# Moving the start of a transformer block's big on-chip tiles by up to 1,472 bytes

## The chip, the core and the metric

The kernel runs on one core of a Trainium2 chip. A core has a matrix engine (TensorE, PE in the profile, with its weight loads shown apart as PEld), a vector engine (VectorE, DVE), a scalar engine (ScalarE, ACT), a general engine (GpSimd, POOL), and a sync engine (SyncE, SP) that issues most of the DMA transfers. Matrix products read both operands from the on-chip memory (SBUF) and write to accumulators (PSUM). The metric is the time of one execution in microseconds, as the median of several runs.

## The reference

The reference is one decoder layer on 1,024 positions of width 1,024, in float32:

```python
h = rms_norm(x, ln_pre_mix[l])
proj = h @ w_in[l]
...
q, k = rope(q, pos), rope(k, pos)
pool_out = multi_scale_pool(u_pool, w_pool[l], pool_scale[l])
attn_out = dilated_attention(q, k, v).reshape(B, S, ATTN_WIDTH)
mix = jnp.concatenate([pool_out, attn_out], axis=-1) @ w_out[l]
x = x + rms_norm(mix, ln_post_mix[l])
h = rms_norm(x, ln_pre_ffn[l])
f = (jax.nn.silu(h @ w_gate[l]) * (h @ w_up[l])) @ w_down[l]
x = x + rms_norm(f, ln_post_ffn[l])
```

The mixer has twelve rotary attention heads of width 64, each under three window-and-stride patterns that are merged by their softmax denominators, and beside them four groups of trailing-window means. The channel mixer (the FFN) has 2,816 hidden channels.

## The kernel before

**Arithmetic.** Every float32 operand of a large product is split in two parts of a reduced float32 type, "high" and "low": ScalarE writes the high part, and VectorE or GpSimd the remainder. Each product is then three matrix products (`PASSES`: high·high, high·low, low·high). A tile of split data therefore holds rows of 512 numbers, 2,048 bytes, of which a matmul reads one row as its moving operand. In the profile's names the moving operand comes first and the weights (the stationary operand) second: `ps_s<-b,fw` moves a row of `b` past weights from `fw`.

**Stages.** (1) The input is loaded and split, and the first projections are made (to about 84 us). (2) Attention, pooling and the remaining projections are interleaved (to about 440 us): scores move `k` past `qh` and `ql`; ScalarE takes exponentials in tiles `pp`; PE transposes `pp` by an identity or a permutation (`idt`, `pmt`, line 279) and the result is split to `ptr`, which moves past the values `v`. (3) The output projection and two norms follow (to about 484 us). (4) Gate and up projections run as a seven-product scheme on 2×2 blocks of the data and of the weights (Strassen and Winograd), in eleven steps j: first a part of the work of steps 0 to 5 (`firsts`), then the rest (`seven`). (5) The down projection does the same (912 us on). Lines 1468 and 1469 name the moving operand of each product:

```python
SEVEN = {"P1": ("A11", "11", "pj"), "P6": ("S2", "T2", "o"), "P2": ("A12", "21", "pj"), "P7": ("S3", "T3", "o"),
         "P5": ("S1", "T1", "s"), "P4": ("A22", "T4", "o"), "P3": ("S4", "22", "s")}
```

"11", "21" and "22" are blocks of the activations themselves, in the tiles `b` (made by `block`, line 1336); T1 to T4 are differences of blocks, in the tiles `tT`. One product of a step, lines 1560 to 1569, is 2 × 4 × 3 = 24 matmuls with 512 columns. `firsts` (lines 1367 to 1400) computes P1 and P2 of steps 0 to 5, 48 matmuls a step. So `b` moves in P1 and P2 in `firsts`, in P3 of every step, and in P1 and P2 of steps 6 to 10.

**Rooms in SBUF.** Tiles come from pools stacked from two ends. Pools without a side grow from the low (left) end: `const`, `wpool` (raw weights `wraw`), `small`, then `con1` and `att` (the attention's `pp`, `ptr`, `v`, `low`, `mix`, early `xraw`, and the last pool weights, `w`); when those two are closed, `ffnl` takes their place and begins where `con1` began (`b`, `rw` for raw FFN weights, `q`, `r3`, and at the end `xe` and half of the result). Pools with `side="right"` grow from the high end: `xg` (`x`, then `z`, `tT`, `op`), `hlp` (`whl`), `qkp` (`k`, `qh`, `ql`), later `mid` (`fw`, `sq`, `p`). Within a pool the big tiles are multiples of 2,048 bytes, so one offset of the pool's start decides the place of all of them within 2,048 bytes.

**Order.** A list of numbers (`PRM`) sets in which order steps are written, and a scheduler puts the instructions of each engine in a fixed order at build time. Each engine works through its own order and waits on semaphores.

Of the kernel before, what the change touches and what calls it, by code (L numbers as in the profile page):

```python
# [8 lines left out]
F32 = mybir.dt.float32  # L9
# [6 lines left out]
P = 128  # L16
# [254 lines left out]
def hybrid_block(ctx: ExitStack, tc: tile.TileContext, xT, w_in, w_v, w_vp, w_pool, w_out, w_gate, w_up, w_down,  # L271
                 g1, g2, g3, g4, pscale, cost, sint, maskA, maskB, quadA, quadB, lsel, ident, perm, band, out):
    nc = tc.nc
# [7 lines left out]
    const = ctx.enter_context(tc.tile_pool(name="const", bufs=1))  # L281
# [19 lines left out]
    def cload(src, shape, name, pool=None, eng=nc.sync):  # L301
        t = (pool or const).tile(shape, F32, name=name)
        eng.dma_start(t, src)
        return t
# [48 lines left out]
    con1 = left.enter_context(tc.tile_pool(name="con1", bufs=1))  # L353
# [8 lines left out]
    for h in range(2):  # L362
        for a in range(2):
            nc.gpsimd.memset(qlow[h][64 - 64 * a:128 - 64 * a, a].bitcast(F32), 0.0)
    ones = const.tile([P, 1], F32, name="ones")
    nc.vector.memset(ones, 1.0)
    warm = qkp.tile([P, 512], F32R, name="warm", tag="rsw", bufs=1)
    nc.vector.memset(warm.bitcast(F32), 0.0)
# [645 lines left out]
        did(("pool", h))  # L1014

    g2s, g3s, g4s = (cload(g, [P, NK], "g%ds" % (n + 2)) for n, g in enumerate((g2, g3, g4)))
    psc = cload(pscale, [P, 2], "psc", con1)

    def emit(*lists):

# [904 lines left out]
```

## Time and profile before

| | |
|---|---|
| median of 3 runs | 1139.48 us (1139.41 to 1140.89) |
| the profiled execution's own time | 1139.3 us |
| its span, first to last instruction | 1137.5 us |
| PE busy | 1120.4 us, 98% of the span |
| weight loads (PEld) | 958.1 us, 84% |
| DVE, ACT, POOL busy | 71%, 49%, 48% |
| granted PE clock over the span | 0.997 |

The profiled execution spends 1.8 us outside its span. Matmuls overlap in the array, so the duration of one (some 390 ns for 512 columns) is longer than the interval from its start to the next one's start, and it is the interval that costs time. The chain of waits lists the work that ended last, piece by piece, with a start, a length and a count; where PE runs without a break, the length divided by the count is that interval.

### The profile page before, as it was taken

The numbers are of one execution on the slowest core, as the hardware profiler recorded it, in microseconds if no ns is written. First come the engines' busy times: TensorE is split into PE (matmuls) and PEld (weight loads), VectorE is DVE, ScalarE is ACT, GpSimd is POOL, SyncE is SP. The second block draws the span as 40 slices with busy tenths as digits, with TensorE's granted clock in tenths as the row PEclk, the third lists the DMA queues.
The fourth block names the chain that finished last, engine by engine and source line by source line (L and its number), as shares of the span: only waits on it lengthen the run. The fifth ranks groups of instructions, "written<-read, shape, count | busy, mean of one in ns | idle before, by whom it ended". The sixth has DMA issues, their size and how long they took to land.

```text
span 1137.5 us, 16902 instructions
## 1 busy us (share of the span) xinstructions
PE 1120.4 (98%) x5922; PEld 958.1 (84%) x5922; DVE 807.6 (71%) x1516; ACT 559.1 (49%) x1068; POOL 550.6 (48%) x481
## 2 busy tenths in 40 slices
PE   9999999999999999999999999999999999999997
PEld 7888999999898888888888878888888888888896
DVE  7967888888998675989777777665676473343684
ACT  7466667666678573965422222322323434344441
POOL 0122646253465222010267667775577897666521
PEclk9999999999999999999999999999999999999999
DMA  8215242414147555773566666433544796566442
GB/s 280 93 70 186 83 141 75 149 57 167 56 131 246 181 200 193 291 254 123 188 231 231 232 231 231 167 141 142 190 167 167 272 351 222 192 203 192 141 149 74
DMA packets 91156, 201.59 MB, mean 177 GB/s; under 512 B 9280, under 2 KB 25152, under 8 KB 89664
## 3 DMA queue, kind: packets, MB, share of 16 engines
q1 hardware_dynamic: 90096, 199.74, 50.2%
q8 instruction: 46, 0.75, 0.3%
q10 hardware_dynamic: 976, 0.79, 0.2%
q14 instruction: 38, 0.31, 0.1%
HBM read 143.61 MB, written 56.89 MB: 176 GB/s over the span
## 4 chain that ended last, share of the span: by engine, by line
PE 87%; DVE 6%; POOL 3%; DMA 2%; issue 1%; ACT 1%; SPq 0%; ACTq 0%; DVEq 0%; POOLq 0%
PE ps_pj L276 28%; PE ps_s L276 25%; PE ps_o L276 22%; PE ps_t L276 10%; PE ps_t L279 3%; DMA rw<-in_w_up_dram 1%; POOL fw L1365 1%; POOL pp L814 1%; DVE pp L748 1%; DVE ptr L860 1%; DVE rsw L510 0%; POOL whl L1464 0%; DMA wraw<-in_w_in_dram 0%; ACT pp L751 0%; DVE ql L542 0%
## 5 line engine op out<-in xcount | busy, mean ns | idle before, releaser
L276 PE MATMUL ps_o<-tT,fw 128*128 128x512 f32 x648 | 150.9, 390 | 0.9 <-DVE sq L1548 0.9
L276 PEld LDWEIGHTS ps_o<-tT,fw 128*128 128x128 f32 x648 | 121.5, 188 | 26.9 <-issue 1.3
L276 PE MATMUL ps_pj<-x,whl 128*128 128x512 f32 x480 | 138.1, 407 | 0.3 <-DVE whl L322 0.3
L814 POOL TENSOR_SCALAR pp<-pp,wv 128x256 f32<-128x256 f32 (+1 forms) x135 | 67.8, 523 | 111.5 <-DVE wv L794 111.5
L1365 POOL TENSOR_TENSOR fw<-rw,fw 128x512 fp32r<-128x512 f32 x72 | 100.3, 1416 | 30.2 <-ACT fw L1363 30.1
L751 ACT ACTIVATE pp<-pp,sx 128x128 f32<-128x128 f32 (+1 forms) x192 | 89.3, 468 | 31.5 <-DVE sx L748 30.9
L276 PEld LDWEIGHTS ps_pj<-x,whl 128*128 128x128 f32 x480 | 85.0, 189 | 11.2 <-DVE whl L322 0.7
L348 POOL TENSOR_TENSOR nrr<-nrr,half 128x4 f32<-128x4 f32 (+1 forms) x7 | 7.9, 1124 | 145.5 <-ACT eps L347 103.8
L1660 POOL TENSOR_TENSOR op<-rw,op 128x512 fp32r<-128x512 f32 x38 | 62.3, 1638 | 32.5 <-ACT op L1659 32.5
L322 POOL TENSOR_TENSOR whl<-wraw,whl 128x512 fp32r<-128x512 f32 x42 | 54.7, 1327 | 45.3 <-ACT whl L318 45.3
L276 PE MATMUL ps_s<-b,fw 128*128 128x512 f32 x312 | 74.6, 394 | 0.0
L276 PEld LDWEIGHTS ps_s<-b,fw 128*128 128x128 f32 x312 | 58.5, 187 | 14.2
L1365 POOL TENSOR_TENSOR whl<-rw,whl 128x512 fp32r<-128x512 f32 x30 | 47.1, 1589 | 44.2 <-ACT whl L1363 30.1
L276 PE MATMUL ps_pj<-whl,x 128*128 128x256 f32 (+1 forms) x432 | 68.4, 299 | 0.0
L1363 ACT ACTIVATE fw<-rw 128x1024 fp32r<-128x1024 f32 x45 | 47.5, 1061 | 41.8 <-PE ps_o L276 17.8
L1659 ACT ACTIVATE op<-rw 128x1024 fp32r<-128x1024 f32 x38 | 40.0, 1058 | 56.4 <-PE ps_t L276 28.2
L860 DVE TENSOR_TENSOR ptr<-ps_t,ptr 128x512 fp32r<-128x512 f32 (+1 forms) x84 | 55.3, 665 | 12.1 <-ACT ptr L859 11.3
L859 ACT ACTIVATE ptr<-ps_t 128x512 fp32r<-128x512 f32 (+1 forms) x84 | 47.4, 578 | 27.9 <-PE ps_t L279 24.0
L276 PEld LDWEIGHTS ps_pj<-whl,x 128*128 128x128 f32 x432 | 58.2, 191 | 1.7
L1661 DVE TENSOR_TENSOR op<-rw,op 128x512 fp32r<-128x512 f32 x33 | 28.8, 872 | 40.1 <-ACT op L1659 29.9
L276 PE MATMUL ps_o<-ptr,v 128*128 128x128 f32 (+1 forms) x472 | 56.4, 257 | 0.2 <-DVE ptr L860 0.2
L276 PE MATMUL ps_s<-k,qh 128*128 128x128 f32 (+1 forms) x192 | 54.4, 295 | 1.9 <-DVE sx L748 1.5
(328 smaller groups left out, 2858.7 us busy)
## 6 DMA issues: line engine op xcount, KB each, us to landing
rw<-bd SPq DMA_DIRECT2D x77, 256.0 KB, 4.0
rw<-in_w_gate_dram SPq DMA_DIRECT2D x28, 512.0 KB, 4.3
rw<-in_w_up_dram SPq DMA_DIRECT2D x28, 512.0 KB, 5.9
v<-vd SPq DMA_DIRECT2D x22, 512.0 KB, 4.6
rw<-wsd SPq DMA_DIRECT2D x44, 256.0 KB, 3.8
bd<-p SPq DMA_DIRECT2D x39, 256.0 KB, 2.1
rw<-in_w_down_dram SPq DMA_DIRECT2D x33, 256.0 KB, 3.8
wraw<-in_w_out_dram SPq DMA_DIRECT2D x15, 512.0 KB, 4.8
```

The source lines that it names most:

```text
L276: return tc.keep_in_program_order(nc.tensor.matmul(*a, **k))
L279: return tc.keep_in_program_order(nc.tensor.transpose(dst, src, by))
L322: pin(eng.tensor_tensor(dst[:, 1, at:at + w], src[:, at:at + w], dst[:, 0, at:at + w].bitcast(F32), ALU.subtract))
L751: nc.scalar.activation(pt[:, j, lo:], pt[:, j, lo:], AF.Exp, bias=sx[:, 0, side, j, hd, 0:1], scale=-1.0, accum_out=sx[:, 0, side, j, hd, ...
L814: nc.gpsimd.tensor_scalar(pv, pv, un.wv[:, side, j, hd:hd + 1], 1.0, op0=ALU.mult, op1=ALU.mult)
L859: nc.scalar.activation(ptr[:, 0, :w], t[:, :w], AF.Copy)
L860: nc.vector.tensor_tensor(ptr[:, 1, :w], t[:, :w], ptr[:, 0, :w].bitcast(F32), ALU.subtract)
L1363: nc.scalar.activation(dst[:, :, 0], src, AF.Copy)
L1365: low[0] = eng.tensor_tensor(dst[:, i, 1], src[:, i], dst[:, i, 0].bitcast(F32), ALU.subtract)
L1659: nc.scalar.activation(w[:, :, 0], raw, AF.Copy)
L1660: nc.gpsimd.tensor_tensor(w[:, 0, 1], raw[:, 0], w[:, 0, 0].bitcast(F32), ALU.subtract)
L1661: (nc.gpsimd if p == "P1" else nc.vector).tensor_tensor(w[:, 1, 1], raw[:, 1], w[:, 1, 0].bitcast(F32), ALU.subtract)
```

## The change

Two small tiles become longer: `ones`, in the pool `const`, from 4 to 1,092 bytes in each partition, and `psc`, in `con1`, from 8 to 392 bytes. Only the first columns are used, as before. The load of `psc` is written out because the helper would load the whole tile; it is the same transfer of 2 numbers at the same place in SP's order.

```diff
-    ones = const.tile([P, 1], F32, name="ones")
+    ones = const.tile([P, 273], F32, name="ones")[:, :1]
     nc.vector.memset(ones, 1.0)
...
-    psc = cload(pscale, [P, 2], "psc", con1)
+    psc = con1.tile([P, 98], F32, name="psc")[:, :2]
+    nc.sync.dma_start(psc, pscale)
```

In the built program no instruction is added, removed or moved on any engine, and every wait is the same. What differs is addresses. All that lies behind `ones` on the left moves up by 1,088 bytes, and all that lies behind `psc` in `con1` and `att` by 384 bytes more. Bytes beyond a multiple of 2,048 at which the tiles begin:

| tiles | side | before | after |
|---|---|---|---|
| `b`, `rw`, `q`, `r3`, `xe` (pool `ffnl`) | left | 928 | 2,016 |
| `pp`, `ptr`, `v`, `xraw`, `w` (pool `att`) | left | 544 | 2,016 |
| `low`, `mix` (pool `att`) | left | 1,568 | 992 |
| `wraw` | left | 832 | 1,920 |
| `pmt`, `idt` | left | 0 and 224 | 1,088 and 1,312 |
| `x`, `z`, `tT`, `op`, `whl`, `fw`, `k`, `qh`, `ql`, `sq`, `p` | right | 2,016 | 2,016 |

## The prediction

> **What bounds the kernel now.** I read the page's totals and chain first, then busy time by stage, then matmuls by operand, then the chain of waits piece by piece.
>
> ```profile
> span 1137.5 us, 16902 instructions
> PE 1120.4 (98%) x5922; PEld 958.1 (84%) x5922; DVE 807.6 (71%) x1516; ACT 559.1 (49%) x1068; POOL 550.6 (48%) x481
> PE 87%; DVE 6%; POOL 3%; DMA 2%; issue 1%; ACT 1%; SPq 0%; ACTq 0%; DVEq 0%; POOLq 0%
> ...
> 484.00:557.00 73.00, 73.00 (x324) 58.99 (x323) 64.35 (x101) 42.31 (x67) 4.79 (x4) 1.00 0.52 188
> 557.00:912.00 355.00, 354.07 (x1552) 289.65 (x1551) 238.26 (x265) 103.16 (x122) 251.13 (x181) 1.00 0.56 201
> 912.00:1094.00 182.00, 182.00 (x816) 150.97 (x815) 93.74 (x108) 76.14 (x78) 121.62 (x74) 1.00 0.65 213
> ```
>
> The last three rows are stages (start and end, length, then busy time of PE, PEld, DVE, ACT, POOL, granted clock, DMA share). PE is the bound: 87% of the chain, and in the gate, up and down projections it stands still for 0.93 us of 610. There an instruction stream that nobody shortens can become faster only if a matmul itself does. So the question is whether a matmul's time depends on where its operand lies. The matmuls by operand, first those that move `b`, which is on the left at 928 bytes beyond a multiple of 2,048, then those that move tiles of the right part at 2,016:
>
> ```profile
> L276 PE MATMUL ps_s<-b,fw 128*128 128x512 f32 x312 | 74.6, 394 | 0.0
> L276 PE MATMUL ps_pj<-b,fw 128*128 128x512 f32 x216 | 51.7, 394 | 0.0
> L276 PE MATMUL ps_pj<-b,whl 128*128 128x512 f32 x120 | 29.4, 396 | 0.0
> L276 PE MATMUL ps_s<-b,whl 128*128 128x512 f32 x48 | 11.5, 394 | 0.0
> L276 PE MATMUL ps_t<-b,op 128*128 128x512 f32 x48 | 11.4, 396 | 0.0
> L276 PE MATMUL ps_t<-b,fw 128*128 128x512 f32 x48 | 11.4, 396 | 0.0
> ...
> L276 PE MATMUL ps_o<-tT,fw 128*128 128x512 f32 x648 | 150.9, 390 | 0.9 <-DVE sq L1548 0.9
> L276 PE MATMUL ps_s<-tT,whl 128*128 128x512 f32 x192 | 45.1, 390 | 0.0
> L276 PE MATMUL ps_pj<-op 128*128 128x512 f32 x99 | 27.8, 389 | 0.0
> ```
>
> Every group that moves `b` has 394 to 396 ns, every group that moves `tT` or `op` 389 or 390, past weights from the same tiles (`fw`, `whl`) and into the same accumulators (`ps_s`). What counts is the interval between starts. The chain of waits gives it, with start, length and count of each piece:
>
> ```profile
> 507.34 11.20 PE ps_s L276 x48
> 518.54 11.20 PE ps_pj L276 x48
> ...
> 746.62 5.44 PE ps_o L276 x24
> 752.07 5.60 PE ps_s L276 x24
> 757.66 5.60 PE ps_pj L276 x24
> 763.26 5.46 PE ps_o L276 x24
> ```
>
> Pieces of 48 are P1 and P2 of `firsts` (`b`): 11.20 / 48 = 233.3 ns. At 746 us stands a P4 (`tT`), then P3 and P1 (`b`), then P6 (`tT`): 5.60 against 5.44 and 5.46 us, or 233.3 against 227.1 ns at their mean of 5.45.
>
> **The change part by part.** It adds, removes and moves no instruction, and no wait; the longer tiles are written no further than before. What it does is to move the left tiles.
>
> *`b` from 928 to 2,016.* It then lies within 2,048 bytes exactly as `tT`, `op` and the weights do, and I take the interval of `tT`. The six groups add up to 312 + 216 + 120 + 48 + 48 + 48 = 792 matmuls, or 33 runs of 24. Each run loses 5.60 − 5.45 = 0.15 us: 33 × 0.15 = 4.95 us. By time, 288 of them are in `firsts` (1.8 us), 144 in P3 of steps 0 to 5 (0.9 us), 360 in steps 6 to 10 (2.25 us). The ends of the value: nothing, if the offset is not the cause, and 33 × 0.16 = 5.3 us, with the fastest row of `tT`. The row nearest to the new place is `tT`, with the same offset, weights and stage, so I take the upper part.
>
> *What that gain meets.* In one place of this stretch PE does wait. The chain of waits there, and from PE's timeline the run of `b` in it and the wait itself:
>
> ```profile
> 635.73 0.71 DVE ps_s L1556
> ...
> 641.45 6.19 DMA rw<-in_w_up_dram
> ...
> 665.81 7.07 DMA rw<-in_w_up_dram
> ...
> 679.52 0.69 DVE sq L1548
> ...
> 680.34 5.72 PE ps_o L276 x24
> ...
> 657.32 5.76 PE L276 MATMUL ps_s<-b,fw 128*128 128x512 f32 x24
> ...
> 680.34 5.04 PE L276 MATMUL ps_o<-tT,fw 128*128 128x512 f32 x21 [0.93 <-DVE sq L1548]
> ```
>
> From 635.7 to 680.3 us the chain runs through DVE, two weight loads and POOL, and PE comes to its wait 0.93 us early. One run of `b` (657.32) lies inside, so its 0.15 us only makes the wait longer: 1.08 us. The runs before 635.7 lie ahead of the chain's own start and are won in full. The stage's 0.93 us of rest are this one wait, so elsewhere PE is never late. If POOL, 71% busy from 557 to 912 us and a piece of this chain, set the pace in all of steps 0 to 5, their six runs of P3 would be lost, 6 × 0.15 − 0.15 = 0.75 us more; that is an end of the range.
>
> *`att` from 544 to 2,016.* Here are two rows of each kind, pool weights `w` (left, 544) and `whl` (right, 2,016) moved past `x` in the same early stage, and the output projection with weights from `b` (left, 928) and from `whl` under the same moving `fw`:
>
> ```profile
> 33.26 2.91 PE L276 MATMUL ps_pj<-whl,x 128*128 128x512 f32 x12
> ...
> 53.43 2.91 PE L276 MATMUL ps_pj<-w,x 128*128 128x512 f32 x12
> ...
> 454.92 5.49 PE ps_s L276 x24
> 460.41 5.44 PE ps_pj L276 x24
> ```
>
> A row at 544 costs what one at 2,016 costs: 2.91 and 2.91 us for twelve. So neither lying on the left nor leaving 2,016 is dear by itself, and 544 to 2,016 should bring nothing. Weights at 928 cost 5.49 against 5.44: 0.05 us for the one such run, which I count as won. For the narrow matmuls of the attention the trace has no pair of offsets:
>
> ```profile
> L276 PE MATMUL ps_o<-ptr,v 128*128 128x128 f32 (+1 forms) x472 | 56.4, 257 | 0.2 <-DVE ptr L860 0.2
> ...
> L279 PE MATMUL ps_t<-pmt,pp 128*128 128x128 f32 x180 | 27.2, 275 | 0.0
> L279 PE MATMUL ps_t<-idt,pp 128*128 128x128 f32 x144 | 21.9, 279 | 2.1 <-POOL pp L814 2.0
> ```
>
> The transposes are the nearest thing to one: `pmt` at 0 and `idt` at 224 move past the same `pp` with 275 and 279 ns, a difference of 4 ns whose sign says nothing of offsets. I bound these 324 transposes at ±4 ns, ±1.3 us, and take nothing, since `ptr` and `v` move together and keep their distance. Where projections move `x` past `whl` between them, both operands stay where they are.
>
> *ACT, DVE, POOL.* ScalarE reads `rw` at 928 and `wraw` at 832 with the same work:
>
> ```profile
> L1363 ACT ACTIVATE fw<-rw 128x1024 fp32r<-128x1024 f32 x45 | 47.5, 1061 | 41.8 <-PE ps_o L276 17.8 <-PE ps_s L276 9.7 <-DMA wsd<-fw 8.9
> L1363 ACT ACTIVATE fw<-wraw 128x1024 fp32r<-128x1024 f32 x9 | 9.5, 1055 | 2.1 <-PE ps_o L276 2.1
> ```
>
> 1061 and 1055 ns, 0.6% apart, in an engine that is idle two thirds of the stage. The cover is PE's unbroken run; without it, 1% of the chain's ACT share would be 0.1 us. Nothing is counted.
>
> *Transfers.* Rows of 4,096 bytes land 1,088 or 1,472 bytes higher; before, `whl` and `fw` at 2,016 received such rows too. Of all transfers only the two loads in the fence above (6.19 and 7.07 us) are worth naming on the chain, so 1% more would be 0.13 us. I take nothing. [...]
>
> *Sum.* −4.95 + 0.15 − 0.05 = −4.85 us on the profiled execution's 1139.3 us: 1134.4 us. That execution lies 0.2 us under the median of the runs, within their spread.
>
> **The rivals.** *The offset is not the cause, and nothing changes.* `b` could be dear because of where it lies in the whole memory, or what it shares with `rw`, which lies beside it and is filled and read all the time. For it: every `b` moved with nothing but one offset, so the trace has no `b` elsewhere. Against it: 233.3 ns alike at 507 us and at 757 us, with POOL at 4.8 of 73 us in the one stage and at 251 of 355 in the other; and `w` on the left at no extra cost. Time: 1139.3 us. [...]
>
> *The attention pays.* What counts may be the distance of a moving row to the weights that are being loaded meanwhile. For `b` that distance goes to that of `tT`; but `idt` and `pmt` against `pp`, and `pp` and `v` against the `x` and `k` around them, get new distances. 472 matmuls of `ptr` past `v` and 324 transposes are 796. From 4.85 us / 796 = 6.1 ns for each the gain is gone; at twice the 0.15 us / 24 = 6.25 ns that `b` pays today the sum is −4.85 + 796 × 12.5 ns = +5.1 us, 1144.4 us. For it: these steps are on PE, which bounds there too. Against it: operands at 2,016 on both sides are what `tT`, `op` and `fw` have, the best rows of the trace.
>
> *Half of it.* The gain of `b` comes, and the early steps 0 to 5, where POOL paces the chain, give their 0.75 us back, and the transposes pay their 1.3 us: 1134.4 + 0.75 + 1.3, or 1136.5 us.
>
> **How the numbers follow.** The forecast, with its own range of 1132.8 (5.3 us of `b`, transposes 1.3 us faster) to 1135.7 us (transposes 1.3 us slower), has 0.78. Half of it has 0.09. No change has 0.09, the attention 0.04. A measurement of this kernel can tell 0.2%, 2.3 us, from no change, so 1137.2 us is the border of "faster": 0.78 and most of the half case give 0.86; no change and the rest give 0.10; slower is 0.04. The range takes the forecast's own and the half case, with 0.2 us on either side, by which the profiled execution differs from the median: 1132.6 to 1136.7 us.
>
> **What would show it.** In the profile after, the six rows that move `b` should read 389 to 391 ns, and the chain's pieces of 48 in `firsts` 10.9 us in place of 11.20. The stage of `firsts` should be 1.8 us shorter, steps 6 to 10 by 2.2 us, and the down projection and all before 484 us unchanged to a few tenths. PE's wait for DVE `sq` at L1548 should grow from 0.9 to 1.1 us. If `b` stays at 394, the first rival holds; if `b` falls and the sum does not, the rows of `ptr`, `idt` and `pmt`, or a longer wait at L1548, must have risen. Wrong by more than the range would be a second effect of the new places in the attention, in either direction.

## The result, and the profile after

| | before | after |
|---|---|---|
| median of 7 runs of each | 1140.36 us (1139.41 to 1141.96) | 1134.72 us (1133.93 to 1138.03) |
| ratio | | 0.9958, 95% interval 0.9944 to 0.9973 |
| the profiled execution's own time | 1139.3 us | 1138.03 us |
| its span | 1137.5 us | 1135.1 us |

The change makes the kernel faster by 0.42% (the interval lies below 1); the forecast was 1134.4 us. The seven runs of the changed kernel lie in two groups, four at 1133.9 to 1134.7 us and three at 1136.9 to 1138.0 us, and the profiled execution is the slowest of the seven. So its rows must be read stage by stage; its end says little. The totals and the share of each engine in the chain, after:

```profile
span 1135.1 us, 16902 instructions
PE 1117.0 (98%) x5922; PEld 959.7 (85%) x5922; DVE 805.9 (71%) x1516; ACT 559.5 (49%) x1068; POOL 550.8 (49%) x481
PE 82%; DVE 5%; POOL 5%; DMA 4%; issue 2%; ACT 1%; SPq 0%; ACTq 0%; DVEq 0%; POOLq 0%
```

The matmuls by operand (count, then busy time and mean ns of one):

```profile
L276 PE MATMUL ps_o<-tT,fw 128*128 128x512 f32 x648 | 150.8, 390 | 0.4 <-DVE sq L1549 0.4
L276 PE MATMUL ps_s<-b,fw 128*128 128x512 f32 x312 | 72.5, 389 | 0.0
L276 PE MATMUL ps_pj<-b,fw 128*128 128x512 f32 x216 | 50.3, 389 | 0.0
L276 PE MATMUL ps_pj<-b,whl 128*128 128x512 f32 x120 | 28.7, 392 | 0.0
...
L276 PE MATMUL ps_s<-b,whl 128*128 128x512 f32 x48 | 11.2, 389 | 0.0
L276 PE MATMUL ps_t<-b,op 128*128 128x512 f32 x48 | 11.0, 389 | 0.0
L276 PE MATMUL ps_t<-b,fw 128*128 128x512 f32 x48 | 11.0, 389 | 0.0
```

All six rows that move `b` fell from 394 to 396 ns to 389 to 392 ns and now read like `tT`. The chain of waits (start, length, count of each piece):

```profile
499.44 10.88 PE ps_t L276 x48
...
746.43 5.44 PE ps_o L276 x24
751.87 5.44 PE ps_s L276 x24
757.31 5.44 PE ps_pj L276 x24
762.75 5.44 PE ps_o L276 x24
```

A piece of 48 in `firsts` went from 11.20 to 10.88 us, one start from 233.3 to 226.7 ns. P4, P3, P1 and P6 in a row now cost the same. The three stages, with their borders laid at the same matmuls as before (start and end, length, busy time of PE, PEld, DVE, ACT, POOL, granted clock, DMA share, GB/s):

```profile
487.49:558.68 71.19, 71.19 (x324) 58.92 (x323) 64.27 (x101) 42.66 (x67) 4.82 (x4) 1.00 0.55 192
558.68:909.57 350.89, 350.54 (x1552) 289.86 (x1551) 236.49 (x265) 103.34 (x122) 251.34 (x181) 1.00 0.56 203
909.57:1091.55 181.98, 181.98 (x816) 150.98 (x815) 94.10 (x108) 76.17 (x78) 121.63 (x74) 1.00 0.66 214
```

`firsts` is shorter by 1.81 us (73.00 before), the rest of gate and up by 4.11 us (355.00), the down projection by 0.02 us. That is 5.9 us won from 484 us on. Of the 4.11 us, 504 starts of `b` at 6.6 ns make 3.3 us, and 0.58 us is a wait of PE near 680 us that was shorter in this execution, of which more below. Ahead of that, by the starts of the same matmuls, this execution was 0.5 us early at 345 us and 3.6 us late at 390 us. The chain between, from the transfer that writes `mix` out to the matmuls that wait for its return as `m`:

```profile
361.63 0.38 SPq L1146
...
362.06 10.15 DMA mixd<-mix
...
372.23 5.93 DMA m<-mixd
...
378.20 4.60 PE ps_pj L276 x12
```

And the granted clock (the third number from the end of a row) just before and behind it, the first stretch holding PE's wait of 2.0 us:

```profile
376.00:378.50 2.50, 0.47 (x3) 0.30 (x2) 1.95 (x10) 0.56 (x2) 0.38 (x1) 1.00 0.80 234
378.50:381.90 3.40, 3.40 (x9) 2.67 (x8) 0.89 (x2) 0.13 (x1) 3.40 (x8) 0.50 1.08 363
```

Before, `m` came in time. Now PE stood for 2.0 us, and for the 3.4 us behind that it ran at half clock: nine matmuls ran there, twenty in the same stretch of the trace before. Half of 3.4 us is 1.7 us, and 2.0 + 1.7 us is nearly all of the loss of 4.1. Whether the moved `mix` had brought that, or chance, was the first thing to find out; the second was what it is about 928 and 2,016 that costs `b` its 6.6 ns a matmul.

### The profile page after: what moved, and what is told of

It is laid out like the page before. It is cut to its first block, busy times and chain, and to the rows that moved or that the text cites. A ratio compares the mean times of both kernels' runs of the same rounds, so it can differ in the third digit from the quotient of the medians.

```text
span 1135.1 us, 16902 instructions
## 1 busy us (share of the span) xinstructions
PE 1117.0 (98%) x5922; PEld 959.7 (85%) x5922; DVE 805.9 (71%) x1516; ACT 559.5 (49%) x1068; POOL 550.8 (49%) x481
## 4 chain that ended last, share of the span: by engine, by line
PE 82%; DVE 5%; POOL 5%; DMA 4%; issue 2%; ACT 1%; SPq 0%; ACTq 0%; DVEq 0%; POOLq 0%
PE ps_pj L276 27%; PE ps_s L276 23%; PE ps_o L276 19%; PE ps_t L276 10%; PE ps_t L279 2%; POOL fw L1366 2%; POOL whl L1465 1%; DMA rw<-in_w_gate_dram 1%; DMA mixd<-mix 1%; POOL pp L814 1%; POOL whl L1366 1%; DMA whl<-in_w_down_dram 1%; DVE pp L748 1%; DMA rw<-in_w_up_dram 1%; DMA m<-mixd 1%
```

## Experiments

Three theories of `b` were open. *The own offset*: a row that begins at 928 is dear wherever the weights lie. *The place*: `b` is dear for its neighbours or its region, and moving it anywhere would change that. *The distance*: what counts is how far the moving row lies from the slices of weights, modulo some power of two. Before, `b` lay 64 bytes short of the weights' phase (928 is 416 beyond a multiple of 512, 2,016 is 480), after at 0. Slices of weights begin 512 bytes apart and rows 2,048 bytes, so each pair of tiles has one such distance.

**One half of the change each, the right part moved in its stead, and the changed kernel again.** These four ran on one chip, beside 17 runs of the kernel before with a median of 1140.68 us (1138.38 to 1144.26).

The feed-forward part's tiles move, and `wraw`, `pmt` and `idt` with them as in the change; the attention's pool goes back to 544:

```diff
     ones = const.tile([P, 273], F32, name="ones")[:, :1]
...
-    psc = con1.tile([P, 98], F32, name="psc")[:, :2]
+    psc = con1.tile([P, 242], F32, name="psc")[:, :2]
```

> The feed-forward part's tiles alone begin at 2,016 (b, rw, q, r3); the attention's tiles stay at 544, mix with them. The theory that b's rows carry the whole gain: b's rows read 389 to 391 ns, a piece of 48 reads 10.9 us, and the time lies 5.0 to 5.3 us under the kernel before (the start-by-start comparison of the two traces gives 5.2 us for the b runs), that is near 1134.6. The rival that the attention's tiles carry part of it: less than 4.5 us are won. On the 2.0 us wait for m that the trace of the changed kernel has near 376 us, with mixd<-mix at 10.2 us in place of 8.5: if it comes from mix at 992, this kernel has no such wait and its times lie together; if it is chance of the transfers, some runs of this kernel too lie some 3 us above the others.

Measured: 1134.86 us (1133.77 to 1135.68, 6 runs), ratio 0.9947, interval 0.9933 to 0.9960. Its rows of `b`, and of `w`, which stayed at 544 and reads as in the kernel before:

```profile
L276 PE MATMUL ps_s<-b,fw 128*128 128x512 f32 x312 | 72.5, 389 | 0.0
...
L276 PE MATMUL ps_pj<-w,x 128*128 128x512 f32 x24 | 6.0, 392 | 0.0
```

`b` alone carries the gain. By medians it is 5.8 us, a little over the 5.0 to 5.3 expected; 5.3 us would be a ratio of 0.9954, inside the interval. Six runs without one near 1137 us, with `mix` back at 1,568, left the question of the wait to the next ones.

Only the tiles of the attention's pool move; `wraw`, `pmt` and `idt` stay:

```diff
-    ones = const.tile([P, 273], F32, name="ones")[:, :1]
+    ones = const.tile([P, 1], F32, name="ones")
...
-    psc = con1.tile([P, 98], F32, name="psc")[:, :2]
+    psc = con1.tile([P, 370], F32, name="psc")[:, :2]
```

> The attention's tiles alone begin at 2,016 (w, band, dhl, xn, with mix at 992); b, rw, q and r3 stay at 928. The theory that b carries the whole gain: b's rows stay at 394 to 397 ns and a piece of 48 at 11.2 us, and the time stays within 1.3 us of the kernel before; the start-by-start comparison gives -0.5 us for the work before 302 us. If mix at 992 is what makes the transfers late, m's wait of some 2 us and the stretch at half clock behind it are there and the time is 2 to 3 us above the kernel before; the rival of my list that the attention pays would make it 5.1 us slower (near 1144.4), as 1144.4 was worked out without b's gain.

Measured: 1139.72 us (1138.43 to 1141.52, 12 runs), ratio 0.9993, interval 0.9983 to 1.0002: no change that can be told.

```profile
L276 PE MATMUL ps_s<-b,fw 128*128 128x512 f32 x312 | 74.6, 394 | 0.0
...
L276 PE MATMUL ps_pj<-w,x 128*128 128x512 f32 x24 | 5.9, 389 | 0.0
```

`b` stays at 394 ns. `w` goes from 392 to 389 ns, so the attention has a little of the same effect: 24 matmuls at 3 ns in this row. By the starts of the same matmuls in the two traces, all work before 302 us won 0.5 us. It pays nothing, and the rival of 1144.4 us falls. The transposes show why, by their starts: the distance of `idt` and `pmt` from `pp` takes the values 0, 32, 64, 96, 192 and 224 (modulo 256) in the kernel before, the changed one and the two halves, and the median interval is 109 ns in all four. Whatever `b` suffers, these matmuls of 128 columns do not. Twelve runs with `mix` at 992 do not reach 2 to 3 us above the kernel before.

The left part as before, and the whole right part moved down to 928:

```diff
-    ones = const.tile([P, 273], F32, name="ones")[:, :1]
+    ones = const.tile([P, 1], F32, name="ones")
...
+    low_by = ctx.enter_context(tc.tile_pool(name="low_by", bufs=1, side="right"))
+    low_by.tile([P, 272], F32, name="pad")
     xgp = ctx.enter_context(tc.tile_pool(name="xg", bufs=1, side="right"))
...
-    psc = con1.tile([P, 98], F32, name="psc")[:, :2]
-    nc.sync.dma_start(psc, pscale)
+    psc = cload(pscale, [P, 2], "psc", con1)
```

> The left part stays as before (b at 928) and an unused pad moves every tile of the right part from 2,016 to 928, the weights that b meets with it. The theory that b's own offset decides (2,016 is good, 928 is bad): b's rows stay at 394 ns, and the some 3,800 matmuls of 512 columns whose moving rows lie on the right slow from 226.7 to 233.3 ns a start, +25 us, near 1164. The theory that only the distance between the moving row and the weights that are loaded beside it counts (here 0 again, in multiples of 512): b's rows read 389 ns with b where it was, those of the right part stay at 389, and the time is near 1134.5. The theory that b's place in memory decides: b at 394 ns, the right unchanged, near 1139.5.

Measured: 1134.80 us (1133.72 to 1135.76, 6 runs), ratio 0.9947, interval 0.9933 to 0.9960, as good as the change itself.

```profile
L276 PE MATMUL ps_o<-tT,fw 128*128 128x512 f32 x648 | 151.3, 390 | 0.8 <-DVE sq L1550 0.8
L276 PE MATMUL ps_s<-b,fw 128*128 128x512 f32 x312 | 72.5, 390 | 0.0
...
L276 PE MATMUL ps_pj<-m,whl 128*128 128x512 f32 x96 | 25.1, 400 | 0.9 <-DMA m<-mixd 0.9
...
L276 PE MATMUL ps_pj<-w,x 128*128 128x512 f32 x24 | 6.1, 395 | 0.0
```

This settles it between the three. `b` was not touched, neither its address nor its neighbours, and reads 390 ns: the place and the own offset fall. `tT` and `fw` are now all at 928 and read 390 ns as ever, where the own offset had asked for 25 us more. And `w`, still at 544 but now 128 from the phase of `x` instead of 64, got slower, 395 ns in place of 392. Here, too, PE waited 0.9 us for `m`, with `mix` where it always was.

The changed kernel again:

> The changed kernel again, nothing else. Its times lay in two groups, near 1134.3 and near 1137.6, and the profiled execution was of the upper one, with the wait of 2.0 us for m near 376 us and 3.4 us at half clock behind it. If the transfers' chance decides, the two groups come again, and a profile of the lower group shows no wait for m; its span is then some 3 us shorter. If the moved mix decides, the wait stands in every execution, and the groups have another cause.

Measured: 1134.47 us (1133.24 to 1135.35, 6 runs), ratio 0.9944, interval 0.9930 to 0.9958. No upper group. The transfers between 360 and 385 us in this trace, and in the first one of the changed kernel (KB each, us from issue to landing):

```profile
mixd<-mix SPq DMA_DIRECT2D x1, 512.0 KB, 9.9
m<-mixd SPq DMA_DIRECT2D x1, 512.0 KB, 3.9
```

```profile
mixd<-mix SPq DMA_DIRECT2D x1, 512.0 KB, 10.2
m<-mixd SPq DMA_DIRECT2D x1, 512.0 KB, 5.9
```

The same program at the same addresses brings `m` back in 3.9 us one time and 5.9 us another. With 3.9 PE does not wait for it at all. So the wait is not `mix`'s new place: it is absent here with `mix` at 992 and present above, shorter, with `mix` at 1,568. It goes with the landing of `m`: 3.7 to 3.9 us in four traces without the wait (this one, the kernel before, and each half alone), 5.2, 5.8 and 5.9 us in the three with it (the right part moved, the fourth map below, and the first trace of the changed kernel). What decides that, I have not found; nor is it shown that the upper group's other two runs had this wait, as they have no trace.

**The law of the distance.** Four kernels put unused pads between the blocks of `b`, so that P1 ("11"), P2 ("21") and P3 ("22") each get a distance of their own from weights that stay at 2,016. The edit, on the changed kernel, with the pads of the first (bytes; key 5 lies ahead of "22", 0 ahead of "11", 2 ahead of "21"):

```diff
+    PADS = {5: 1984, 0: 1600, 2: 576}
...
+        if PADS.get(n):
+            ffnl.tile([P, PADS.pop(n) // 4], F32, name="pad%d" % n, tag="pad%d" % n)
         return ffnl.tile(shape, dt, name=name, tag="b%d" % n)
```

The other three differ in that line alone: `{5: 1920, 0: 1152, 2: 1152}`, `{5: 256, 0: 1760, 2: 64}` and `{5: 320, 0: 1824, 2: 64}`.

> The changed kernel with unused pads between the tiles of the seven products, so that the three operand sums lie at three distances from the weights' slices (which begin at 2,016, so at 480 in every 512): b of 22 (moving rows of P3) at 1,952, -64; b of 11 (P1) at 1,504, a whole 512 away, so 0; b of 21 (P2) at 32, +64. The theory of the distance modulo 512: P3's rows read 394 ns and start 233.2 ns apart as before, P1's stay at 389 ns and 226.7 although b lies at another place in 2,048, P2's lie between, near 229 ns a start, as the rows of fw past b4 do in the kernel before. The rival of the distance modulo 2,048 (or of the own offset): P1 slows too. Time: 264 matmuls x 6.5 ns and 264 x 2.3 ns over the changed kernel, +2.3 us, near 1136.8; the rival some 1.7 us more.

> As the map with 64, with b of 22 at 1,888 (-128), b of 11 at 992 (1,024 away: 0 by 512), b of 21 at 96 (+128). The theory of the distance modulo 512: P1 stays at 226.7 ns a start; P3 and P2 are slower than 226.7, by an amount that no row shows yet: w moved by +128 in the kernel with the right part moved costs 2.5 ns a start more than at +64, so P2 near 231 to 234, P3 at 233 or above. The rival that only a short distance (a conflict of neighbouring rows) costs: both back at 226.7. Time between 1134.5 and 1138.5 by these.

> As the map with 64, with b of 22 at 224 (+256, the farthest there is by 512), b of 11 at 1,984 (-32), b of 21 at 0 (+32). The theory of the distance modulo 512 says that +256 is slowest or, if the pattern has a period of 256, back at 226.7; -32 and +32 lie between 226.7 and the values at 64 (230 and 228). A period of 64 would have shown nothing at 64, so if -32 and +32 are free the step lies between 32 and 64. Time between 1134.5 and 1138.5.

> The changed kernel with the pads set so that b of 22 (P3) lies at 288 (+320 by the distance from the weights' slices, so 64 beyond a whole 256), b of 11 (P1) at 64 (+96), b of 21 (P2) at 128 (+160). Seen so far, a start: 0 and 256 226.7 ns, +32 and -32 233.4, +64 229.6, -64 233.3, +128 and -128 233. The theory of a period of 256: P3 reads what +64 did, 229 to 230 ns; P1 and P2 near 233. The rival of a period of 512 with 256 free by its own: P3 near 233. Time: 264 matmuls x 2.9 ns and 528 x 6.3 ns over 1134.5, so near 1138.6 by the first, 1139.6 by the second; a single run scatters by as much, so the rows decide.

Measured, one run each, on two other chips: 1136.28, 1137.31, 1139.56 and 1140.94 us (the kernel before beside them, one run each, 1139.76 and 1140.18 us). The chain of each, in that order, first a piece of 48 in `firsts` (P1 and P2 in turn), then a P3:

```profile
517.84 11.00 PE ps_pj L276 x48
...
574.07 5.60 PE ps_s L276 x24
```

```profile
517.95 11.05 PE ps_pj L276 x48
...
574.29 5.59 PE ps_s L276 x24
```

```profile
520.40 11.20 PE ps_pj L276 x48
...
577.21 5.44 PE ps_s L276 x24
```

```profile
522.07 11.22 PE ps_pj L276 x48
...
578.92 5.51 PE ps_s L276 x24
```

With P1 and P2 taken apart by the starts in the traces, and distances counted modulo 256:

| distance of the moving row from the weights | where | ns of one | ns from start to start |
|---|---|---|---|
| 0 | all of `b` after; P3 at +256 | 389 | 226.7 |
| 32 | P2 in the third map | 395 | 233.4 |
| 64 | P2 in the first; P3 at +320 in the fourth | 392 | 229.6 |
| 96 | P1 in the fourth | 396 | 233.7 |
| 128 | P2 and P3 in the second | 395 | 233.0 |
| 160 | P2 in the fourth | 396 | 233.9 |
| 192 | `b` before; P3 in the first | 394 | 233.3 |
| 224 | P1 in the third | 396 | 233.4 |

P1 in the first two maps, 512 and 1,024 bytes off, reads 228 ns on average. In the first map its run behind a slower P2 in `firsts` starts with ten intervals of 225 to 236 ns, and the rest are 226 or 227: the slower spacing outlasts its cause by some ten starts. So the period is 256 bytes, as far as these kernels reach: P3 at +256 takes 5.44 us for 24, as at 0, and at +320 it takes 5.51, the 229.6 ns of +64. Of the distances tried, all multiples of 32, only 0 is free; 64 costs 2.9 ns a start, less than half of the rest; all others cost 6.3 to 7.2 ns. My third expectation was wrong to put 32 between: it costs as much as 128. The end times follow where nothing else happens (first map: 1136.8 expected, 1136.28 measured). The third lies above its expected 1134.5 to 1138.5 us: its trace is 1.8 us late within the first 10 us, before any `b` (PE pauses of 0.85 and 0.69 us, and the clock at half from 8.2 us on). The fourth had PE's wait for `m` again, 1.6 us and a stretch at half clock behind it, so its 1140.94 us says nothing.

The distance counts the other way round as well. In the output projection `fw` moves past weights from the `b` tile that the first pad shifts. That row before, after, and in the second, third and fourth map:

```profile
L276 PE MATMUL ps_s<-fw,b 128*128 128x512 f32 x24 | 5.7, 391 | 0.0
```

```profile
L276 PE MATMUL ps_s<-fw,b 128*128 128x512 f32 x24 | 5.6, 389 | 0.0
```

```profile
L276 PE MATMUL ps_s<-fw,b 128*128 128x512 f32 x24 | 5.8, 395 | 0.0
```

```profile
L276 PE MATMUL ps_s<-fw,b 128*128 128x512 f32 x24 | 5.6, 389 | 0.0
```

```profile
L276 PE MATMUL ps_s<-fw,b 128*128 128x512 f32 x24 | 5.8, 396 | 0.0
```

Their distances are 64, 0, 128, 256 (that is 0) and 192: the table's values, though here the moving row never moved.

No kernel of these beats the changed one; the changed kernel, the one with `b` alone, and the one with the right part moved can't be told apart (1134.47, 1134.86 and 1134.80 us). They share what matters: in every product of the feed-forward part both operands begin at the same bytes modulo 256.

## Why the prediction came out as it did

**`b`, 33 runs at 0.15 us = 4.95 us: right, and a little short.** 24 matmuls went from 5.60 to 5.44 us, so a run is worth 0.16 us and 33 runs 5.28 us; from the starts, 792 × (233.3 − 226.7) ns = 5.2 us. The prediction took the mean of 5.44 and 5.46 for `tT`. That P6 of 5.46 us stood behind a run of `b`, its first five intervals 225 to 236 ns; it is 5.44 after. `firsts` was to win 1.8 us and won 1.81.

**The reason given with it was only half of it.** The step said that `b` would lie "exactly as `tT`, `op` and the weights do", and took the offset as the cause; the first rival was "the offset is not the cause". The kernel with the right part moved shows that 928 is not dear by itself: `tT` past `fw`, both there, reads 390 ns as at 2,016. The distance stood in the prediction, too, but as the attention's threat. That the two readings give the same number here is luck of the case: had the change moved the weights along with `b`, the step would still have forecast a gain, and by the distance there would have been none.

**`att` from 544 to 2,016, counted at nothing: a small gain instead.** The pair of rows that read 2.91 us each compared `w` at distance 64 with `whl` at 0 and concluded that 544 costs nothing. But the row of `whl` was itself disturbed: its first seven starts lie 224 to 236 ns apart and only the last five 226 or 227, while `w` keeps to 230 on average. The same two rows after, `whl` as before and `w` shorter:

```profile
33.22 2.91 PE L276 MATMUL ps_pj<-whl,x 128*128 128x512 f32 x12
...
53.22 2.88 PE L276 MATMUL ps_pj<-w,x 128*128 128x512 f32 x12
```

Over the 24 of the row shown above `w` read 392 ns before, 389 after, 395 at distance 128. The term was mis-sized by at most 0.5 us, the gain of all work before 302 us; with `b` alone or the right part moved, where `w` did not come to 0, the same work won 0.2 and 0.1 us, so 0.3 to 0.4 us go with the move. All 48 matmuls of `w` at 3.4 ns make 0.2 us of it; the rest is not traced. The ±1.3 us for the transposes was bounded by durations (275 and 279 ns), where the prediction itself held that starts count: these have a median of 109 ns for both. The weights at 928, 0.05 us, came as said: that run reads 389 after 391 ns.

**The wait at L1548, 0.93 to grow to 1.08 us: wrong.** It fell. The chain of the changed kernel, and from PE's timeline the wait itself:

```profile
667.03 6.26 DMA rw<-in_w_up_dram
...
679.94 0.69 DVE sq L1549
```

```profile
680.76 5.73 PE L276 MATMUL ps_o<-tT,fw 128*128 128x512 f32 x24 [0.35 <-DVE sq L1549]
```

The last weight load took 6.26 us in place of 7.07, 0.8 us less, and the wait shrank by 0.58 us; the rest of that chain starts elsewhere in it, too. In the kernel where only the attention moved, with `b` as before, PE waited 0.4 us at the same place. So the step that failed is the assumption that this chain's length is fixed. It holds a transfer whose time varies by more than the 0.15 us that I followed through it.

**Transfers, ACT, DVE, POOL at nothing: right for the addresses, wrong for the scatter.** The wait for `m`, the one followed here, did not go by an address. But its 2.0 us, and the half clock behind it, moved this one execution by 3.7 us, more than half of the change, and no term of the sum and no rival had it. The median held; three of the ten traces have such a wait, of 0.9 to 2.0 us.

**The rivals.** No change (1139.3 us) falls with every row of `b`: with the same instructions and waits a start takes 226.7 ns after and took 233.3 ns before, by the distance of the two operands alone. The attention's rival named the right quantity, the distance, and the wrong price: `w` became cheaper, and the transposes cost the same. "Half of it" asked that steps 0 to 5 give 0.75 us back; their stage won in full.

The sum that the runs support: −5.2 us for `b` and −0.3 to −0.5 us for the work before 302 us, −5.5 to −5.7 us together, where I had −4.85. The medians differ by 5.6 us in the first comparison and by 6.2 us in the repeated one.

## What to carry to other kernels

Where matmuls of 512 columns follow each other without a gap, compare, for each pair of moving and stationary tile, the two start addresses modulo 256 before you look for anything dearer: here it made 792 matmuls 2.8% faster from start to start, at the price of some unused bytes. Here it didn't matter which side was moved (`b` reads 389 ns with the left part moved, 390 with the right one), or by how much, once the difference was a multiple of 256 (226.7 ns a start at 0 and at +256). The transposes of 128 columns did not show the effect (109 ns a start at six distances), and other widths were not looked at. And when one profiled execution contradicts the median, look for a wait on a transfer that other executions of the same program do not have (here `m`, landing in 5.9 us in one and 3.9 in another), before explaining it by the change.

## What the hardware showed that I had not expected

*The distance itself*, 0 (226.7 ns a start) against anything else tried (233.0 to 233.9), with 64 in between (229.6) and a period of 256 bytes. Why, these runs do not show: all weights of a product have the same phase, so it is not told apart whether a row meets its own weights or the next ones being loaded. Nor do they show why a run at distance 0 behind a slower one needs some ten starts to come back to 227 ns.

*After a short pause of PE its clock was often at half for 3.4 us.* All ten traces have a pause of 2.0 us near 351 us, where PE waits for POOL. In eight the clock is 0.50 for 3.4 us soon after it; in two, the kernel with the attention's tiles alone moved and the one with the right part moved, it is not. The PE timeline of the first of the two at the pause, and its busy times and clock (third from the end) in the stretch behind:

```profile
352.96 1.05 PE L279 MATMUL ps_t<-idt,pp 128*128 128x128 f32 x4 [1.96 <-POOL pp L814]
```

```profile
352.90:356.40 3.50, 3.42 (x23) 3.06 (x24) 3.38 (x7) 1.61 (x3) 3.50 (x7) 1.00 0.89 317
```

The stretch behind the pause in the second:

```profile
353.40:356.90 3.50, 3.42 (x23) 3.06 (x24) 3.38 (x7) 1.58 (x3) 3.50 (x7) 1.00 0.88 301
```

The pause and the stretch behind it in the repeated run of the changed kernel:

```profile
353.21 1.05 PE L279 MATMUL ps_t<-idt,pp 128*128 128x128 f32 x4 [1.96 <-POOL pp L814]
```

```profile
354.90:358.30 3.40, 3.40 (x18) 3.40 (x17) 3.34 (x8) 1.72 (x4) 3.40 (x6) 0.50 0.95 357
```

The clock fell after the waits for `m` of 2.0 and 1.6 us, too, and not after the one of 0.9 us. At two of the ten pauses of 1.03 us near the end of the kernel it fell as well, at 1122.9 us in the repeated run of the changed kernel and at 1124.7 us with the right part moved. So the half clock followed nine of the eleven pauses of 2.0 us, the one of 1.6 us, none of 0.9 us, and two of the ten of 1.03 us. The wait of 2.0 us for `m` cost some 3.7 us in this way, an estimate from its own length and half of 3.4 us. Behind the pause near 351 us, among matmuls of 128 and 256 columns, the half clock cost less: the two traces without it gain some 0.5 us on the kernel before between 345 and 360 us.

Whether the clock falls is one of the things in which executions of one program differ. In each trace it changes only at whole multiples of 3.413 us after the first clock record (348.16 us, 102 of them, from 5.00 to 353.16 us in the kernel before, and as many from 6.44 to 354.60 us in the changed one), and that record lies anywhere from 4.8 to 6.9 us in the ten traces, so the same pause meets this grid at another place each time. That this decides is not shown.
